# Strided attention: one store for two groups instead of one for each

## The chip, the cores and the metric

The kernel runs on one core of a Trainium2 chip. The metric is the device time of one execution in microseconds (us). The kernel before took 128.28 us, the median of three runs from 128.15 to 128.48.

## The reference

Every one of the 1024 queries of a head attends to the same 16 keys: positions 0, 64, 128, ... There are 8 x 12 = 96 heads with 64 elements per row, all in float32.

```python
attend_positions = np.arange(0, seq, stride)          # stride = 64, so 16 keys
q = Q[:, :, i:i + 1, :]
k = K[:, :, attend_positions, :]
v = V[:, :, attend_positions, :]
scores = np.einsum('bhqd,bhkd->bhqk', q, k) * scale   # scale = 1 / 8
weights = np.exp(scores - np.max(scores, axis=-1, keepdims=True))
weights = weights / (np.sum(weights, axis=-1, keepdims=True) + 1e-10)
result[:, :, i, :] = np.einsum('bhqk,bhkd->bhqd', weights, v)[:, :, 0, :]
```

Little is computed for each byte: 25.2 MB of Q are read, 25.2 MB of results are written, and of K and V only 0.8 MB together.

## The kernel before

The 96 heads are worked on in 24 groups of four heads. One group is 1 MiB of Q and 1 MiB of output. The four heads of a group follow one another in HBM.

For a group g the steps are these. `load(g)` brings Q into one of ten buffers `qn`; groups 0 and 1 come as 128 rows of 8 KiB, the others as 32 rows of 32 KiB. `cast(g)` turns it to bf16, half on GpSimd (L196) and half on ScalarE (L197). `transpose(g)` (VectorE, L206) turns 32 x 32 blocks of pairs. `scores(g)` is four matmuls (L219) and two exponentials on ScalarE (L231). `values(g)` lays the group's values out for the matmul (GpSimd, L184). `outputs(g, c)` with c = 0, 1, 2 multiplies weights and values (L247), takes the reciprocal of the sums (VectorE, L255) and scales into the output buffer: VectorE for c = 0 and 1 (L257), ScalarE and then GpSimd for c = 2 (L259, L260). The GpSimd instruction at L260 is the last one of a group. `store(g)` writes the group out.

In an output buffer a partition holds 8 KiB in a row: 4 x 8 rows of 64 elements, in all 2048 of float32. In HBM these 8 KiB are two pieces of 4 KiB, 512 KiB apart (pattern `[2 * SD, 2], [1, 16 * D]`). There are eight output buffers, so group g writes where group g-8 stood.

The order is written out by hand; no scheduler moves anything. In the loop, step g first runs `ahead(g)`: the transpose of group g+2, the scores of g+1, the values of g+2 and the cast of g+3. Then come the outputs of g, then `store(g)`, then `load(g + 10)`. The transpose of group g waits for the store of group g-10, since VectorE soon writes into that buffer.

All transfers are issued by SyncE (SP), in program order, on one queue: K, Q of group 0, V, Q of groups 1 to 9, and then store 0, load 10, store 1, load 11 and so on to store 13 and load 23, then stores 14 to 23 alone. An issue of a store waits for the L260 of its group; what stands behind it on SyncE waits with it. Completion is told by eight semaphores used in turn, so each issue also waits until the transfer eight issues earlier has landed.

Of the kernel before, what the change touches and what calls it, by code (L numbers as in the profile page):

```python
# [10 lines left out]
FP32 = mybir.dt.float32  # L11
# [6 lines left out]
def _ap_with(ap: bass.AP, new_ap, extra_offset: int = 0) -> bass.AP:  # L18
    return dataclasses.replace(
        ap, ap=[list(p) for p in new_ap], offset=ap.offset + extra_offset  # L20
    )


def _copy(nc, out: bass.AP, in_: bass.AP):

    sides = [
        mybir.BassSymbolicTensorAccessPattern(
            ap=side.ap, dtype=side.dtype, bass_ap=side,
            is_dma=True, for_custom_bir_dma=True,
        )  # L30
        for side in (in_, out)
    ]
    return nc.sync.add_instruction(
        mybir.InstDMACopy(
            name=nc.get_next_instruction_name(), engine=mybir.EngineType.SP,
            ins=sides[:1], outs=sides[1:], queue="qSPDynamicHW",
            mode="Copy",
        )
    )
# [9 lines left out]
def kernel(  # L49
# [10 lines left out]
    B, H, S, D = Q.shape  # L60
# [3 lines left out]
    P = 128  # L64
    HG = 4
    NG = B * H // HG
    NC = NG // 2
    SD = S * D
    KW = P + NK
    assert B * H == NG * HG and S == 1024 and D == 64 and NK == 16  # L70
    QBUFS = 10
    OBUFS = 8

    const = ctx.enter_context(tc.tile_pool(name="const", bufs=1))
# [12 lines left out]
    identity = const.tile([P, P], BF16, name="identity")  # L87
    qn_bufs = [const.tile([P, 32 * D], FP32, name=f"qn{i}") for i in range(QBUFS)]
    qb_bufs = [const.tile([P, 32 * D], BF16, name=f"qb{i}") for i in range(2)]
    out_bufs = [const.tile([P, 4, 8, D], FP32, name=f"out_sb{i}") for i in range(OBUFS)]  # L90
    kv_src = [[stride * D, P], [2 * HG * SD, NC], [1, D]]
    qn, stored, cast_by, scaled = {}, {}, {}, {}
    loaded, raised, masked = {}, {}, {}

    def implied(ins, earlier, why):
        tc.declare_no_dep(ins.ins, earlier.ins, reason=why)

    def load(g):
        qn[g] = qn_bufs[g % QBUFS]
        n = P if g < 2 else 32  # L100
        loaded[g] = _copy(nc, qn[g], _ap_with(Q, [[HG * SD // n, n], [1, HG * SD // n]], g * HG * SD))
        if g >= QBUFS:
            for earlier in (loaded[g - QBUFS], *cast_by[g - QBUFS]):
                implied(loaded[g], earlier, "the store before it has waited for both casts")
# [4 lines left out]
    for g in range(1, QBUFS):  # L109
# [13 lines left out]
        out=identity, in_=identity, compare_op=ALU.not_equal, fill=1.0, base=0,  # L123
# [3 lines left out]
    for c in range(2):  # L127
        for a in range(2):
            nc.gpsimd.tensor_copy(
                out=perm_v[:, c, a],  # L130
# [6 lines left out]
        out=s_sel, in_=identity.rearrange("p (h s k) -> p s h k", h=2, s=4),  # L137
# [10 lines left out]
    def key_rows(part):  # L148
        nc.scalar.copy(k_bf[:, part], k_raw[:, part])  # L149
        nc.vector.transpose(  # L150
            k_r[:, part].rearrange("p n d -> p (n d)").bitcast(I32),
            k_bf[:, part].rearrange("p n d -> p (n d)").bitcast(I32),
        )


    def keys(part, c, s):
        src, dst, col = 32 * (2 * c + s % 2), 32 * (2 * (s % 2) + s // 2), NK + 32 * s
        op = nc.gpsimd.tensor_copy if part is first and s >= 2 else nc.scalar.copy
        op(  # L159
            k_t[dst : dst + 32, 2 * part.start + c : 2 * part.stop : 2, :, col : col + NK],  # L160
            k_r[src : src + 32, part].rearrange(
                "p n (a k f) -> p a n f k", a=2, f=2
            )[:, s // 2],
        )


    def value_rows(n):
        vp = psum_o.tile([P, 3, 512], FP32, name="o_ps", tag="o")
        rows = vp[:, 0:2, 0 : NC // 2 * D].rearrange("p c (n d) -> p c n d", d=D)
        for c in range(2):  # L170
            nc.tensor.matmul(  # L171
                rows[:, c], lhsT=perm_v[:, c].rearrange("p a b e k -> p (a b e k)"),
                rhs=v_bf[:, 6 * n : 6 * n + 6], start=True, stop=True,
            )
        nc.vector.tensor_copy(  # L175
            out=v_rep[:, 6 * n : 6 * n + 6].rearrange("p n c d -> p c n d"), in_=rows
        )

    qb, qt, wt, vb, rec, out_sb = {}, {}, {}, {}, {}, {}
# [59 lines left out]

    def outputs(g, c):  # L240
        if c == 0:
            out_sb[g] = out_bufs[g % OBUFS]
            rec[g] = rec_pool.tile([P, 8, 4], FP32, name="rec", tag="rec")
        i0, n = ((0, 3), (3, 2), (5, 3))[c]
        ps = psum_o.tile([P, 3, 512], FP32, name="o_ps", tag="o")
        for i in range(n):
            nc.tensor.matmul(  # L247
                ps[:, i, 0 : 4 * D + 4], lhsT=wt[g][:, i0 + i], rhs=vb[g],
                start=True, stop=True,
            )  # L250
        r = rec[g][:, i0 : i0 + n]
        o = ps[:, 0:n, 0 : 4 * D].rearrange("p i (s d) -> p i s d", s=4)
        to = out_sb[g][:, :, i0 : i0 + n].rearrange("p s i d -> p i s d")
        by = r.unsqueeze(3).to_broadcast([P, n, 4, D])
        nc.vector.reciprocal(r, ps[:, 0:n, 4 * D : 4 * D + 4])  # L255
        if c < 2:
            nc.vector.tensor_tensor(out=to, in0=o, in1=by, op=ALU.mult)  # L257
        else:
            copied = nc.scalar.copy(to, o)  # L259
            scaled[g] = nc.gpsimd.tensor_tensor(out=to, in0=to, in1=by, op=ALU.mult)  # L260
            for past in range(g - OBUFS, -1, -OBUFS):
                for earlier in (stored[past], scaled[past]):
                    implied(copied, earlier, "VectorE has waited for the store")
                implied(scaled[g], stored[past], "VectorE has waited for the store")

    def store(g):
        o = out_sb[g]
        stored[g] = _copy(
            nc,
            _ap_with(out, [[16 * D, P], [2 * SD, 2], [1, 16 * D]], g * HG * SD),  # L270
            _ap_with(o, [o.ap[0], [1, 1], [1, 32 * D]]),
        )

    first, rest = slice(0, 4), slice(4, NC)
    key_rows(first)
# [15 lines left out]
    def ahead(g):  # L291
        if g + 2 < NG:
            transpose(g + 2)
        if g + 1 < NG:
            scores(g + 1)
        if g + 2 < NG:
            values(g + 2)
        if g + 3 < NG:
            cast(g + 3)

    for g in range(NG):
        if g > 0:
            ahead(g)
        for c in range(3):
            outputs(g, c)
        if g == 0:
            ahead(g)
        if g == 1:
            key_rows(rest)
        if 2 <= g < 6:  # L310
            for i in range(2 * g - 4, 2 * g - 2):
                keys(rest, i // 4, i % 4)
        if g == 4:
            value_rows(1)
        store(g)
        if g + QBUFS < NG:
            load(g + QBUFS)
# [1 line left out]
_INS = ['Q', 'K', 'V', 'stride']  # L319
_OUTS = [((8, 12, 1024, 64), 'float32')]  # L320
# [30 lines left out]
```

## Time and profile before

| | before |
|---|---|
| median of three runs | 128.28 us (128.15 to 128.48) |
| the profiled execution | 128.42 us |
| its span | 126.3 us |
| bytes moved | 51.19 MB, mean 405 GB/s over the span |
| busy: PE, DVE, ACT, POOL | 51%, 68%, 67%, 62% of the span |
| a Q load, issue to landing (median) | 14.8 us |
| a store, issue to landing (median) | 15.3 us |
| SyncE waiting before L33 | 37.7 + 24.9 + 12.6 + 12.1 us for GpSimd and transfers |

The profile is one execution. PE is TensorE, DVE is VectorE, ACT is ScalarE, POOL is GpSimd, SP is SyncE, and SPq is SyncE issuing. The span runs from the first to the last instruction; the 2.1 us that the execution takes beyond it lie around the program. A digit in the slices is the busy share of 3.2 us in tenths. A line of a window gives its bounds, its length, the busy time and count of each engine, the granted clock, the share of the 16 DMA engines' time that packets took (packets count in the window where they start, so it can pass 1), and the rate. A line of issues gives start, duration, engine, line, output and input. The number at the end of a line of DMA issues is the time from issue to landing.

Beside these views the trace keeps a record of every packet, with start, duration and size, and of every time that an engine's share of a transfer landed. Of the 7904 packets on the queue 3072 are K's and V's rows of 256 bytes, 800 are the 4-byte writes that tell of completion (16 for each of 50 transfers), 3328 have 8 KiB and 704 have 32 KiB.

### The profile page before, as it was taken

The numbers are of one execution on the slowest core, as the hardware profiler recorded it, in microseconds if no ns is written. First come the engines' busy times: TensorE is split into PE (matmuls) and PEld (weight loads), VectorE is DVE, ScalarE is ACT, GpSimd is POOL, SyncE is SP. The second block draws the span as 40 slices with busy tenths as digits, with TensorE's granted clock in tenths as the row PEclk, the third lists the DMA queues.
The fourth block names the chain that finished last, engine by engine and source line by source line (L and its number), as shares of the span: only waits on it lengthen the run. The fifth ranks groups of instructions, "written<-read, shape, count | busy, mean of one in ns | idle before, by whom it ended". The sixth has DMA issues, their size and how long they took to land.

```text
span 126.3 us, 1113 instructions
## 1 busy us (share of the span) xinstructions
PE 64.3 (51%) x292; PEld 29.8 (24%) x292; DVE 85.8 (68%) x151; ACT 84.5 (67%) x111; POOL 78.1 (62%) x89
## 2 busy tenths in 40 slices
PE   0005279294638776666464977636665459530000
PEld 0001033141313323333231433313333214210000
DVE  5931573659968879797997897979797973660000
ACT  4172807976999999979799768997979493530000
POOL 4084346736766876979979778796968775144000
PEclk9999999968997569999999657999999955965555
DMA  2999989999998998979999989989989899999991
GB/s 63 371 345 467 498 374 457 436 394 384 449 496 340 490 426 363 511 327 441 454 392 433 470 376 462 465 361 490 423 369 501 353 423 418 428 433 420 420 423 67
DMA packets 7910, 51.19 MB, mean 405 GB/s; under 512 B 3872, under 2 KB 3872, under 8 KB 3872
## 3 DMA queue, kind: packets, MB, share of 16 engines
q1 hardware_dynamic: 7904, 51.12, 97.0%
q8 instruction: 2, 0.03, 0.1%
q14 instruction: 4, 0.03, 0.1%
HBM read 25.95 MB, written 25.17 MB: 405 GB/s over the span
## 4 chain that ended last, share of the span: by engine, by line
DMA 37%; DVE 20%; ACT 11%; PE 9%; POOL 8%; issue 3%; SPq 1%; POOLq 1%; DVEq 0%
DMA qn<-in_Q_dram 37%; DVE out_sb L257 10%; DVE qt L206 6%; PE sc L219 4%; ACT out_sb L259 4%; PE o_ps L247 4%; POOL out_sb L260 3%; ACT w_all L231 3%; DVE rec L255 3%; ACT qb L197 3%; POOL qb L196 2%; POOL v_all L184 2%; POOLq L346 1%; DVE v_rep L175 1%; PE o_ps L171 1%
## 5 line engine op out<-in xcount | busy, mean ns | idle before, releaser
L247 PE MATMUL o_ps<-v_all,w_all 128*128 128x260 bf16 x192 | 38.3, 318 | 36.6 <-DVE out_sb L257 31.3
L260 POOL TENSOR_TENSOR out_sb<-out_sb,rec 128x768 f32<-128x768 f32 x24 | 35.3, 1472 | 27.2 <-ACT out_sb L259 27.2
L257 DVE TENSOR_TENSOR out_sb<-o_ps,rec 128x768 f32<-128x768 f32 (+1 forms) x48 | 39.6, 824 | 1.6
L231 ACT ACTIVATE w_all<-sc 64x512 bf16<-64x512 f32 x48 | 35.2, 734 | 5.2 <-PE sc L219 4.7
L206 DVE STREAM_TRANSPOSE qt<-qb 128x1024 int32<-128x1024 int32 x24 | 29.6, 1235 | 11.9 <-POOL qb L196 7.6
L219 PE MATMUL sc<-qt,k_t 128*128 128x512 bf16 x96 | 32.3, 470 | 9.9 <-DVE qt L206 9.9
L247 PEld LDWEIGHTS <-w_all 128*128 128x128 bf16 x192 | 18.8, 109 | 59.5 <-DVE out_sb L257 39.7
L259 ACT COPY out_sb<-o_ps 128x768 f32<-128x768 f32 x24 | 19.2, 799 | 16.3 <-DVE rec L255 15.7
L197 ACT CAST qb<-qn 128x1024 bf16<-128x1024 f32 x24 | 25.0, 1045 | 2.7 <-DMA qn<-in_Q_dram 2.2
L196 POOL CAST qb<-qn 128x1024 bf16<-128x1024 f32 x24 | 24.9, 1038 | 3.0 <-DMA qn<-in_Q_dram 2.9
L255 DVE RECIPROCAL rec<-o_ps 128x12 f32<-128x12 f32 (+1 forms) x72 | 15.0, 209 | 5.7 <-PE o_ps L247 5.2
L184 POOL TENSOR_TENSOR v_all<-mask,v_rep 128x256 bf16<-128x256 bf16 x24 | 16.0, 670 | 1.9 <-DVE v_rep L175 1.9
L219 PEld LDWEIGHTS <-k_t 128*128 128x128 bf16 x96 | 10.6, 111 | 19.9 <-POOL k_t L159 7.5
L159 ACT COPY k_t<-k_r 32x256 bf16<-32x256 bf16 (+1 forms) x12 | 4.4, 366 | 1.3 <-DVE k_r L150 1.1
L175 DVE CAST v_rep<-o_ps 128x768 bf16<-128x768 f32 x2 | 1.9, 958 | 4.6 <-PE o_ps L171 4.6
L133 DVE MEMSET k_t<- 128x3456 uint32 x1 | 2.9, 2938 | 1.5 <-PEq L332 1.5
L149 ACT CAST k_bf<-k_raw 128x256 bf16<-128x256 f32 (+1 forms) x2 | 1.0, 513 | 2.9 <-DMA k_raw<-in_K_dram 2.9
L140 POOL COPY v_all<-s_sel 128x12 bf16<-128x12 bf16 x1 | 0.2, 194 | 4.1 <-DVE s_sel L136 4.1
L171 PE MATMUL o_ps<-v_bf,perm_v 128*128 128x384 bf16 x4 | 1.3, 416 | 1.7 <-POOL v_bf L284 1.4
L149 ACT ACT_TABLE_LOAD x1 | 1.3, 1283 | 0.7 <-PEq L332 0.7
L150 DVE STREAM_TRANSPOSE k_r<-k_bf 128x128 int32<-128x128 int32 (+1 forms) x2 | 0.7, 370 | 1.4 <-ACT k_bf L149 1.4
L134 DVE MEMSET w_all<- 128x1536 uint32 x1 | 1.3, 1338 | 0.3 <-issue 0.3
(12 smaller groups left out, 4.6 us busy)
## 6 DMA issues: line engine op xcount, KB each, us to landing
qn<-in_Q_dram SPq DMA_DIRECT2D x24, 1024.0 KB, 14.8
out_dram<-out_sb SPq DMA_DIRECT2D x24, 1024.0 KB, 15.3
k_raw<-in_K_dram SPq DMA_DIRECT2D x1, 384.0 KB, 4.2
v_raw<-in_V_dram SPq DMA_DIRECT2D x1, 384.0 KB, 6.8
```

What stands on the lines that cost most here:

```text
L159: op(k_t[dst : dst + 32, 2 * part.start + c : 2 * part.stop : 2, :, col : col + NK], k_r[src : src + 32, part].rearrange("p n (a k f) -> p ...
L184: masked[g] = nc.gpsimd.tensor_tensor(out=vb[g][:, 0 : 4 * D].rearrange("p (s d) -> p s d", s=4), in0=mask, in1=v_rep[:, g // 2, g % 2].un ...
L196: nc.gpsimd.tensor_copy(out=qb[g][:, 0:half], in_=qn[g][:, 0:half]),
L197: nc.scalar.copy(qb[g][:, half:], qn[g][:, half:]),
L206: turned = nc.vector.transpose(qt[g].bitcast(I32), qb[g].bitcast(I32))
L219: nc.tensor.matmul(sc, lhsT=k_t[:, g, f, NK * (1 - e) : NK * (1 - e) + P], rhs=_ap_with(q, [q.ap[0], [D, 8], [16 * D, 2], [2, 32]], extra_ ...
L231: raised[g].append(nc.scalar.activation(out=_ap_with(wa, [wa.ap[0], [P, 8], [1, 2], [2, 32]], extra_offset=64 * a), in_=sc[64 * a : 64 * a ...
L247: nc.tensor.matmul(ps[:, i, 0 : 4 * D + 4], lhsT=wt[g][:, i0 + i], rhs=vb[g], start=True, stop=True,)
L255: nc.vector.reciprocal(r, ps[:, 0:n, 4 * D : 4 * D + 4])
L257: nc.vector.tensor_tensor(out=to, in0=o, in1=by, op=ALU.mult)
L259: copied = nc.scalar.copy(to, o)
L260: scaled[g] = nc.gpsimd.tensor_tensor(out=to, in0=to, in1=by, op=ALU.mult)
```

## The change

The eight output buffers become four of two groups each: a partition holds 16 KiB in a row, the lower group first. Group 0 lies alone in the second half of the first buffer, then come the pairs (1,2), (3,4) to (21,22), and group 23 lies alone in a first half. Still a group writes where the group eight before it stood.

A pair is stored by one transfer of 2 MiB, after its second group is done: 128 rows of 16 KiB out of the buffer, in HBM four pieces of 4 KiB each, 512 KiB apart. The two loads of the pair follow it. So the queue is now store 0, load 10, store (1,2), loads 11 and 12, and so on to store (11,12), loads 21 and 22, store (13,14), load 23, four more pairs and store 23. There are 39 transfers in place of 50. The eight semaphores still limit how many are under way.

```diff
-    out_bufs = [const.tile([P, 4, 8, D], FP32, name=f"out_sb{i}") for i in range(OBUFS)]
+    out_bufs = [const.tile([P, 2, 4, 8, D], FP32, name=f"out_sb{i}") for i in range(OBUFS // 2)]
...
-            out_sb[g] = out_bufs[g % OBUFS]
+            out_sb[g] = out_bufs[(g + 1) // 2 % (OBUFS // 2)][:, (g + 1) % 2]
...
-    def store(g):
-        o = out_sb[g]
-        stored[g] = _copy(
+    def store(lo, hi):
+        n, pair = hi + 1 - lo, out_bufs[(hi + 1) // 2 % (OBUFS // 2)]
+        o = pair[:, (lo + 1) % 2]
+        done = _copy(
             nc,
-            _ap_with(out, [[16 * D, P], [2 * SD, 2], [1, 16 * D]], g * HG * SD),
-            _ap_with(o, [o.ap[0], [1, 1], [1, 32 * D]]),
-        )
+            _ap_with(out, [[16 * D, P], [2 * SD, 2 * n], [1, 16 * D]], lo * HG * SD),
+            _ap_with(o, [o.ap[0], [1, 1], [1, n * 32 * D]]),
+        )
+        for g in range(lo, hi + 1):
+            stored[g] = done
...
-        store(g)
-        if g + QBUFS < NG:
-            load(g + QBUFS)
+        if g % 2 == 0 or g == NG - 1:
+            lo = max(g - 1, 0) if g % 2 == 0 else g
+            store(lo, g)
+            for past in range(lo, g + 1):
+                if past + QBUFS < NG:
+                    load(past + QBUFS)
```

Nothing is changed in the instructions of the other engines, other than the place in memory that the outputs are written to and the stores that the transposes wait for.

## The prediction

> **What bounds the kernel now.** I read the page's slices and queue table first, then transfer rates in windows, then SyncE's issues and the end of the chain of waits.
>
> ```profile
> span 126.3 us, 1113 instructions
> ...
> DMA  2999989999998998979999989989989899999991
> ```
> ```profile
> q1 hardware_dynamic: 7904, 51.12, 97.0%
> ...
> qn<-in_Q_dram SPq DMA_DIRECT2D x24, 1024.0 KB, 14.8
> out_dram<-out_sb SPq DMA_DIRECT2D x24, 1024.0 KB, 15.3
> ```
>
> The reader is to see that the 16 DMA engines hold packets of this one queue for 97.0% of the span (122.5 us), while no compute engine passes 68%. Taking the trace's packet records one by one, all 16 engines hold a packet from 2 to 123 us; the first starts at 1.84, the last ends at 124.98. So the time is the packets' sum. A change helps if it shortens that sum and hurts if it lets the queue run dry; work on the compute engines counts only through when it releases transfers.
>
> ```profile
> core 0: us, PE busy (x) PEld busy (x) DVE busy (x) ACT busy (x) POOL busy (x), PEclk, DMA share, GB/s
> 13.00:27.00 14.00, 8.56 (x29) 3.51 (x29) 8.70 (x14) 8.63 (x11) 7.10 (x9) 0.96 1.01 433
> 103.00:115.00 12.00, 6.12 (x25) 2.51 (x23) 6.62 (x16) 4.87 (x7) 6.05 (x5) 0.64 1.01 425
> ```
>
> The first window holds only loads of 32 rows of 32 KiB, the second only stores of 128 rows of 8 KiB. At the same share the short rows move 2% less.
>
> ```profile
> 21.42 0.63 SPq L33 DMA_DIRECT2D out_dram<-out_sb  x1
> 22.10 0.60 SPq L33 DMA_DIRECT2D qn<-in_Q_dram  x1
> 28.87 0.59 SPq L33 DMA_DIRECT2D out_dram<-out_sb  x1
> 29.51 0.69 SPq L33 DMA_DIRECT2D qn<-in_Q_dram  x1
> 33.91 0.59 SPq L33 DMA_DIRECT2D out_dram<-out_sb  x1
> ...
> 42.24 0.59 SPq L33 DMA_DIRECT2D out_dram<-out_sb  x1
> ```
> ```profile
> 81.22 19.52 DMA qn<-in_Q_dram
> ...
> 110.72 1.47 POOL out_sb L260
> 112.20 1.48 issue
> 113.68 1.51 POOLq L346
> ```
>
> The first list has stores 0, 1 and 2 and their loads: early on SyncE issues when a group is done. The second says that the last load lands at 100.74, that group 22 is done at 112.20 and group 23 at 115.2; store 23 is issued there and lands 10 us later, behind three others.
>
> **The change, part by part.** *Packets.* Eleven pairs are stored as rows of 16 KiB. In the packet records an 8 KiB store packet takes 311 ns (median) and a 32 KiB load packet 1219 ns from 55 us on: four starts against one cost 4 x 311 - 1219 = 25 ns, 8.3 ns a start. The windows agree: 425 and 433 GB/s over 16 engines at 1.01 are 311.5 and 305.7 ns per 8 KiB, and 5.8 ns is three quarters of a start of 7.7 ns. An engine has 8 of a store's 128 rows, so 88 starts fall away: 88 x 8.3 = 0.73 us. No row shows a 16 KiB packet. The upper end is the rate of the 32 KiB packets, 176 x 5.8 = 1.02 us. The lower end is below nothing: an HBM row of a store is 4 KiB, so a 16 KiB packet jumps three times where two of 8 KiB jump once each, and 8 KiB stores at 311 against the one-piece 8 KiB loads at 309 give 2 ns a jump: 88 x 2 = 0.18 us lost if nothing is merged. I take 0.73, because the 32 KiB load is also a packet of four pieces on its far side, the nearest form.
>
> A rule prices the same step lower. The Trainium skill (DMA: Bandwidth & Descriptors, Why small descriptors are slow) gives about three cycles of overhead per packet; at the 850 MHz of its section Where 436 GB/s comes from that is an estimated 3.5 ns, so 88 x 3.5 = 0.31 us, and the sum would be 0.4 us higher, about 128.1. The 8.3 ns of this trace disagree, so I keep those.
>
> *Completion writes.* Each transfer ends in one 4-byte packet per engine, 9 ns in the records. Eleven fewer: 0.10 us.
>
> *SyncE.* Eleven issues of 0.59 us go. SyncE spends 88 us of the span in waits before L33, so this is worth nothing on the path; the queue behind it is what covers it.
>
> *Store g waits for g+1 (g odd), and so do its load and everything behind it on SyncE.* The worst place is the first pair. Load 10, issued at 22.10, lands at 35.68 on its last engine and about 35.0 on its first; by the records the engines are free from 34.68 to 35.32. Before, store 1 and load 11 (29 us) were queued behind it. Now nothing is until store (1,2) at 33.91, when group 2 is done. How long from issue to first packet on an empty queue? One row: K is issued at 0.74 and its first packet starts at 1.84, 1.10 us. With SyncE's 0.59 for a store instead of K's 0.43 it is 1.26, so about 35.2. An engine idles 0 to 0.5 us; bound above by K's landing at 4.2 us less its 1.73 us of packets and 0.4 of landing, 2.1 us from issue, which is 36.0 and a gap of 0.7 to 1.3 us. Below, nothing. I take 0.2 us, the nearest row being K's start.
>
> The next pair: from 35.2, a pair (16 x 0.307 = 4.9 us) and loads 11 and 12 (2.44 each) run to 45.0. Group 4 is done at 42.24 and its store starts by 43.5. Ahead by 1.5 us, then 2.6 at group 6, and more after, since groups finish every 3.3 to 4.3 us and transfers need 4.9 a group. So this happens once.
>
> *Loads.* Load 10+g of an odd g now stands behind store g+1: 2.46 us later in the queue; even ones keep their place. Casts come long after their loads until about load 20, so those delays are covered. The last, load 23, is odd: it lands 2.46 later less 0.5 us saved on seven pairs by then, near 102.7. The chain after it is rigid (11.5 us to group 22, 14.4 to group 23): 114.2 and 117.1.
>
> *The end.* Store (21,22) is issued at 114.2 and starts by 115.5. The store ahead of it, (19,20), ends where store 20 did less about 0.7: 115.0 on the first engine and 116.9 on the last (records: 115.70 and 117.59). The early engines may idle 0.5 us, but they had 1.5 us to spare on the late one that sets the end. Store 23 comes at 117.1, before (21,22) ends at 119.9 or later. Cost nothing; that cover goes if the first packet needs 2.7 us.
>
> *Buffers.* Still eight groups deep. The transpose of group g waits for the store of g-10, which for odd g now lands with its partner; but in the queue that store still stands ahead of load g, which the same transpose needs. Nothing.
>
> *Sum.* 128.42 (the profiled execution, span 126.3 and 2.1 around it) - 0.73 - 0.10 + 0.20 = 127.8. That execution was 0.14 above the median of 128.28, so against the median 127.65 us.
>
> **Rivals.** *No merging.* If the packets stay at 8 KiB, or the far side's 4 KiB pieces are what costs, 0.10 is gained, up to 0.18 lost, 0.2 lost to the gap: 128.2 to 128.6. For it: the store's HBM rows are 4 KiB. Against: today's packets are 8 KiB, the buffer's row and not the 4 KiB one.
>
> *The queue runs dry* at (1,2), the one that ends slower. Each us that the first packet comes after 35.3 is paid by all engines. The gain of 0.83 is used up when it comes near 36.1, 2.2 us after issue; beyond 36.5 the kernel is slower by over 0.3%. At the 36.0 bound it gives 128.28 - 0.83 + 0.7 to 1.3 = 128.2 to 128.8. Against: K started in 1.10 us. For: that was a load with nothing in flight, and no store has been seen on an empty queue.
>
> *Four pieces half a MiB apart per packet* go slower than two of two. If each of two added jumps cost as much as a packet's start, a packet takes 622 + 17 ns and 88 x 17 = 1.5 us are lost: 128.28 + 1.5 - 0.1 + 0.2 = 129.9. Against: 311 and 309 ns for two pieces and one. The Trainium skill (DMA: Bandwidth & Descriptors, Latency and other measured facts) has copies at a row pitch of 512 KiB at 207 GB/s against 214 with a padded pitch; the stores of this trace already step by 512 KiB and keep 425.
>
> **How the numbers follow.** Merging with a small gap 0.64 (with both unknown costs 128.28 - 1.12 = 127.16 to 128.28 - 0.83 + 0.5 = 127.95), no merging 0.13, dry queue 0.15, slow pieces 0.08. The runs before spread 128.15 to 128.48, so 0.3%, 0.38 us, is what can be told: the first case is faster but for 0.05; no merging is the same, with 0.02 slower; dry splits into 0.08 same and 0.07 slower; slow pieces are slower but for 0.02. Faster 0.59, same 0.26, slower 0.15. The range goes from the low end of the first case, with the runs' scatter 127.1, to 128.7, which takes in no merging and most of the dry case.
>
> **What would show it.** Right: packets of the queue fall from 7904 to 7904 - 1408 - 176 = 6320, the window of pure stores moves 427 to 430 GB/s, the queue's time falls by 0.8 us, the slices near 35 us stay at 9, load 23 lands near 102.7. Wrong: 7728 packets (no merging), a slice under 8 near 35 us (dry), or under 425 GB/s in the last stores (slow pieces).

## The result and the profile after

The changed kernel takes 131.57 us, the median of four runs from 130.73 to 131.84, beside 128.33 us for four runs of the kernel before. The ratio is 1.0236, with a 95% interval from 1.0205 to 1.0267: slower by 2.4%. The forecast was 127.65 us, and 131.57 lies above its range.

The page after, in the lines that answer to those shown of before:

```profile
span 129.7 us, 1090 instructions
...
DMA  2999999999799979999999989989989999998990
```
```profile
q1 hardware_dynamic: 6320, 51.12, 95.3%
...
qn<-in_Q_dram SPq DMA_DIRECT2D x24, 1024.0 KB, 15.2
out_dram<-out_sb SPq DMA_DIRECT2D x11, 2048.0 KB, 14.9
out_dram<-out_sb SPq DMA_DIRECT2D x2, 1024.0 KB, 9.8
```

The packets fell to 6320, just as forecast, so the rows did become 16 KiB. But 95.3% of 129.7 us are 123.6 us of packets an engine, against 122.5 before: 1584 packets fewer (1408 rows and 176 completion writes), and over 1 us more. The profiled execution took 131.84 us, 3.42 more than that of before; its last packet ends at 128.38 in the packet records, 3.40 later than before, so all of the loss lies in the transfers.

The rates in three stretches say where. The columns are as in the windows shown before: the last two are the DMA share and GB/s. First the kernel before, then the changed one.

```profile
34.00:46.00 12.00, 8.55 (x37) 3.85 (x35) 9.54 (x16) 11.69 (x18) 8.70 (x9) 0.73 0.95 403
46.00:70.00 24.00, 13.75 (x79) 6.93 (x78) 21.29 (x40) 21.52 (x27) 20.10 (x21) 0.99 1.01 425
70.00:100.00 30.00, 18.88 (x95) 9.20 (x93) 25.78 (x49) 24.83 (x31) 24.09 (x24) 0.89 1.01 426
```
```profile
34.00:46.00 12.00, 7.21 (x40) 3.27 (x38) 10.63 (x20) 11.45 (x18) 8.45 (x10) 0.98 0.93 350
46.00:70.00 24.00, 14.94 (x72) 7.18 (x72) 20.12 (x38) 21.45 (x28) 19.66 (x20) 0.86 0.99 413
70.00:100.00 30.00, 16.97 (x84) 8.37 (x84) 23.39 (x43) 22.30 (x29) 21.33 (x21) 0.88 1.01 423
```

Between 34 and 46 us the changed kernel moves 53 GB/s less, 0.64 MB or 1.5 us of work at 425 GB/s. Between 46 and 70 it is 12 GB/s, 0.7 us. The DMA share falls by only 0.02 in both, so most of this is not an idle queue: packets take longer. (The share counts a packet that is held up as busy.)

SyncE's issues of the changed kernel (start, duration, engine, line, output and input):

```profile
22.04 0.60 SPq L33 DMA_DIRECT2D qn<-in_Q_dram  x1
34.23 0.59 SPq L33 DMA_DIRECT2D out_dram<-out_sb  x1
34.86 1.96 SPq L33 DMA_DIRECT2D qn<-in_Q_dram  x2
42.78 0.59 SPq L33 DMA_DIRECT2D out_dram<-out_sb  x1
```

Store (1,2) is issued at 34.23, and by the packet records its first packet starts at 35.48; the engines had been free since 34.56 to 35.16, so the mean engine idles 0.67 us. (The records name no engine. Figures for one engine come from putting packets in chains, each starting where another has just ended.) Then comes what was not forecast. The first six packets of the store on each engine take 608 to 648 ns (616 is the median of 16 KiB packets), the last two up to 1199, and then load packets of 32 KiB, usually 1213 to 1219 ns, take up to 1765. Over the whole kernel, 73 of 704 load packets pass 1260 ns (18 before), in sum 23 us beyond 1218 ns each; long 16 KiB packets add 14 us. Summed over 16 engines that is 2.3 us for each, and some engines carry more than others.

The end of the chain of waits:

```profile
81.95 24.74 DMA qn<-in_Q_dram
...
116.54 1.47 POOL out_sb L260
118.01 1.49 issue
119.50 1.50 POOLq L352
```

Load 23 lands at 106.70, where 102.7 was forecast, and groups 22 and 23 end 11.3 and 14.3 us behind it, at 118.0 and 121.0. Store (21,22) is issued at 118.04, when the first engine has been through with (19,20) since 117.65, so the early engines idle a second time, some 0.7 us on the mean. The latest engine, which sets the end, is never idle there: it leaves (19,20) at 121.01, 3.4 us behind the first (1.9 before).

### The profile page after: what moved, and what is told of

It reads as the page before. It is cut to its first block, busy times and chain, and to the rows that moved or that the text cites. A ratio compares the mean times of both kernels' runs of the same rounds, so it can differ in the third digit from the quotient of the medians.

```text
span 129.7 us, 1090 instructions
## 1 busy us (share of the span) xinstructions
PE 67.5 (52%) x292; PEld 31.1 (24%) x292; DVE 86.1 (66%) x151; ACT 84.7 (65%) x111; POOL 78.1 (60%) x89
## 3 DMA queue, kind: packets, MB, share of 16 engines
q1 hardware_dynamic: 6320, 51.12, 95.3%
## 4 chain that ended last, share of the span: by engine, by line
DMA 26%; DVE 22%; ACT 18%; PE 11%; POOL 10%; issue 3%; SPq 1%; POOLq 1%; DVEq 0%
DMA qn<-in_Q_dram 26%; DVE out_sb L257 11%; DVE qt L206 7%; ACT out_sb L259 6%; ACT w_all L231 5%; PE o_ps L247 5%; PE sc L219 5%; ACT qb L197 5%; POOL out_sb L260 5%; DVE rec L255 3%; POOL qb L196 3%; POOL v_all L184 2%; ACT k_t L159 2%; POOLq L352 1%; DVE v_rep L175 1%
## 5 line engine op out<-in xcount | busy, mean ns | idle before, releaser
L247 PE MATMUL o_ps<-v_all,w_all 128*128 128x260 bf16 x192 | 40.0, 331 | 39.3 <-DVE out_sb L257 29.9
L219 PE MATMUL sc<-qt,k_t 128*128 128x512 bf16 x96 | 33.7, 487 | 9.9 <-DVE qt L206 9.9
L247 PEld LDWEIGHTS <-w_all 128*128 128x128 bf16 x192 | 19.4, 113 | 63.1 <-DVE out_sb L257 38.6
L259 ACT COPY out_sb<-o_ps 128x768 f32<-128x768 f32 x24 | 19.2, 798 | 15.8 <-DVE rec L255 15.6
L219 PEld LDWEIGHTS <-k_t 128*128 128x128 bf16 x96 | 11.3, 117 | 21.0 <-issue 8.3
```

Of the source, the lines that this page charges most:

```text
L219: nc.tensor.matmul(sc, lhsT=k_t[:, g, f, NK * (1 - e) : NK * (1 - e) + P], rhs=_ap_with(q, [q.ap[0], [D, 8], [16 * D, 2], [2, 32]], extra_ ...
L247: nc.tensor.matmul(ps[:, i, 0 : 4 * D + 4], lhsT=wt[g][:, i0 + i], rhs=vb[g], start=True, stop=True,)
```

## The experiments

Three theories were put to test. A: the queue runs empty near 35 and 118 us, and the restart brings the long packets. B: packets of 16 KiB in four pieces hold up the loads beside them. C: two loads back to back bring the long packets; the kernel before alternates one store and one load. In all of them the ratio is to the kernel before on the same chip (128.4 to 128.5 us).

**Order without delay.** Each group is stored alone again; only the order of the changed kernel stays, two stores and then two loads. SyncE issues store 1 when group 1 is done (29.10 us), so nothing is delayed but the first load of a pair.

```diff
-            store(lo, g)
+            for one in range(lo, g + 1):
+                store(one, one)
```

> The order and the delay of the changed kernel, but each group stored by its own transfer of 8 KiB rows: both stores of a pair when its second group is done, then both loads. Theory A (the queue runs empty near 35 us and near 118 us, and the long packets follow from all engines restarting together): as slow as the changed kernel, 131 to 132 us, with an empty stretch of 0.5 us or more near 35 us and single load packets of over 1.4 us after it. Theory B (packets of 16 KiB in four pieces hold up the loads beside them): only the empty stretches stay, 0.7 us each on the mean engine, so 129.0 to 129.7 us, and no more long load packets than before (18).

Measured: 130.15 us, ratio 1.0132 (1.0098 to 1.0166). The expected stop was not there, since store 1 is not held: the engines are not idle between 4 and 124 us. Still 56 load packets are long, with 15.8 us of excess. They fall on both loads of a pair, with three quarters of the excess (11.9 us) on the second. So theory A is not all of it, and B cannot be, since no packet has 16 KiB. That gave theory C.

The excess is 1.0 us an engine, and by the records of completion the mean engine's last share lands 0.8 us later than in the kernel before. The last engine's lands 1.9 us later, and that one sets the time. Why it is so far behind is seen in the page's queue table, in a row that is the same for both kernels:

```profile
q8 instruction: 2, 0.03, 0.1%
```

These are two packets of 16 KiB of instructions. In both kernels the first, near 48 us, takes its place between two packets of the queue on one engine, for 1.18 us before and 1.03 here, and that engine is the last from then on to the end. Here it also has 2.9 us of long packets, the most of all engines, against 0.8 before: together 2.0 us more, where the end came 1.9 us later.

**The rows in 8 KiB, all else as changed.** 256 bytes between the two groups keep the rows apart.

```diff
-    out_bufs = [const.tile([P, 2, 4, 8, D], FP32, name=f"out_sb{i}") for i in range(OBUFS // 2)]
+    out_bufs = [const.tile([P, 2, 33, D], FP32, name=f"out_sb{i}") for i in range(OBUFS // 2)]
...
-            _ap_with(o, [o.ap[0], [1, 1], [1, n * 32 * D]]),
+            _ap_with(o, [o.ap[0], [33 * D, n], [1, 32 * D]]),
```

> As the changed kernel, one transfer for two groups issued at the same place, but the two groups lie 256 bytes apart in the buffer, so that the rows are 8 KiB again. Theory A: 131 to 132.5 us, the empty stretches are the same and the 0.7 us of packet starts are not saved. Theory B: 129 to 130 us, because the packets are those of the kernel before.

Measured: 131.56 us, ratio 1.0244 (1.021 to 1.0277), as expected by theory A, with 75 long load packets and again 350 GB/s from 34 to 46 us. The changed kernel's median is 131.57, but its runs spread over 1.1 us, so that the two agree to 0.01 us is chance. No gain or harm of the rows' length is seen: theory B falls. For the 0.73 us that were to be gained the pace of packets, further down, is the sharper test.

**No stop, merged pairs.** The loads are issued two groups earlier.

```diff
-            for past in range(lo, g + 1):
+            for past in range(lo + 2 if g else 0, g + 3):
```

> Merged pairs of 16 KiB rows as in the changed kernel, but every load after the first ten is issued two groups earlier: loads 10, 11, 12 after store 0, loads 13, 14 after store (1,2) and so on; the queue then holds 4.9 us more work at 35 us and load 23 comes before store (13,14). Theory A: no empty stretch, load 23 near 96 us, and the 0.8 us of the prediction are gained: 127.3 to 127.9 us. Theory B: the 16 KiB packets are all there, so the long load packets stay and only 0.7 to 1.4 us come back: 130 to 131 us.

Measured: 129.55 us, ratio 1.0066 (1.0032 to 1.0099). The queue is not empty near 35 us. 2.0 us come back, more than the 0.7 to 1.4 of theory B, but not all that theory A expected. Loads still come in twos (and three after store 0), and 41 load packets are long with 12.3 us of excess.

**Single groups up to 6**, then pairs:

```diff
-        if g % 2 == 0 or g == NG - 1:
-            lo = max(g - 1, 0) if g % 2 == 0 else g
+        if g % 2 == 0 or g == NG - 1 or g < 7:
+            lo = g - 1 if g % 2 == 0 and g > 6 else g
```

> Groups 0 to 6 stored alone, each followed by its load, as before; pairs of 16 KiB rows from (7,8) to (21,22), group 23 alone. Theory A: the queue is not empty near 35 us, no restart, few long packets; the end has load 23 2.5 us late as predicted: 127.5 to 128.3 us. Theory B: eight of eleven pairs still hold up loads, the pairs beside loads being (7,8) to (13,14), so about 130 us, with long load packets between 60 and 100 us.

Measured: 128.94 us, ratio 1.0037 (1.0018 to 1.0056). No stop near 35 us, and before 70 us only four long load packets. Those that come, 29 with 9.5 us of excess, lie at 70 us and later, where loads come in twos; near 116 us the mean engine idles 0.2 us. It costs half a us still, against the gain that theory A expected, and 1 us less than theory B did.

**Delay without the order.** The pair goes out in rows of 16 KiB after its second group, as even and odd partitions, each half followed by one load. The transposes wait for both halves.

```diff
...
-            store(lo, g)
-            for past in range(lo, g + 1):
+            parts = [slice(0, P, 1)] if lo == g else [slice(0, P, 2), slice(1, P, 2)]
+            for past, part in zip(range(lo, g + 1), parts):
+                store(lo, g, part)
```

> As the changed kernel, still only after the second group of a pair and in rows of 16 KiB, but a pair goes out as two transfers of 1 MiB, one of the even and one of the odd partitions, and each is followed by one of the two loads: store half, load, store half, load, as the kernel before alternates. Theory C (two loads back to back, with all engines reading for 5 us, bring the long load packets): the long packets fall to about the 18 of before, the empty stretch near 35 us stays, and the time is 128.4 to 129.2 us. Theory A (the empty stretch and the restart after it bring them): they stay near 73 and the time is 131 to 132 us.

Measured: 130.2 us, ratio 1.0137 (1.012 to 1.0155), between the two expectations. The stop is there (0.51 us on the mean engine) and so is a burst of long packets right behind it: 13.8 us of excess in the first stores and 16.0 us in load 11. After that, with one store and one load in turn, loads 12 to 23 have 2 us of excess, no more than the kernel before. So there are two causes: a burst after the stop, and long loads where two of them stand in a row.

**Delay alone, in 8 KiB rows** shows the same without halves. The first store of a pair is held until the second group is done; one store and one load in turn.

```diff
-            lo = max(g - 1, 0) if g % 2 == 0 else g
-            store(lo, g)
-            for past in range(lo, g + 1):
+            for past in range(max(g - 1, 0) if g % 2 == 0 else g, g + 1):
+                store(past, past)
+                if past < g:
+                    tc.add_manual_dep(
+                        stored[past].ins, scaled[g].ins.name,
+                        mybir.DependencyInfo(mybir.DependencyClass.Sync, mybir.DependencyReason.ANTI),
+                        reason="held until the second group of the pair is done",
+                    )
                 if past + QBUFS < NG:
                     load(past + QBUFS)
```

> Delay alone: groups stored one by one in rows of 8 KiB, store and load in turn as in the kernel before, but the first store of each pair is held until the second group of the pair is done. If the stop of the queue near 35 us and its restart are what the delay costs: 129.8 to 130.4 us, as with the halves, with 20 us or more of excess in packets between 35 and 46 us. If the halves or their 16 KiB rows had a part in those 1.8 us: under 129.5 us.

Measured: 130.89 us, ratio 1.0182 (1.0164 to 1.02), half a us above the expected range, so the halves and their rows had no part in the loss. Its three stretches:

```profile
34.00:46.00 12.00, 6.87 (x38) 3.28 (x38) 10.76 (x20) 11.62 (x18) 8.63 (x10) 1.00 0.98 355
46.00:70.00 24.00, 14.38 (x75) 7.19 (x76) 20.89 (x39) 21.65 (x28) 19.91 (x21) 0.93 0.98 413
70.00:100.00 30.00, 16.77 (x94) 8.45 (x92) 23.95 (x45) 23.19 (x30) 22.67 (x22) 0.97 1.02 434
```

The packets are those of the kernel before, in its order; only their time differs, and the stretch from 34 to 46 us falls from 403 to 355 GB/s. By the packet records store 1 starts at full pace after the stop; then, on all 16 engines, its last two packets take some 300 ns more than 311 and the one before them 97 to 261 more, and 14 of the 16 second packets of load 11 take 1936 to 2211 ns in place of 1218. From 35 to 45 us that is 13.2 us of excess in stores and 14.1 in loads, 1.7 us an engine; with 0.40 us of idle time 2.1 of the 2.4 us that were lost.

**The transfers alone.** Is it the engines at work beside the transfers? Four kernels leave all computation out: the output buffers are zeroed once, and the zeros are stored. Each ran once, so their times stand for one execution. First the changed kernel's order and rows. Of its loop this is left:

```diff
+    for buf in out_bufs:
+        nc.vector.memset(buf, 0.0)
...
     for g in range(NG):
-        if g > 0:
-            ahead(g)
-        for c in range(3):
-            outputs(g, c)
...
         if g % 2 == 0 or g == NG - 1:
```

> All transfers of the changed kernel in its order (pairs in rows of 16 KiB, then two loads), and no computation: the output buffers are zeroed once and stored, the result is not attention. The queue is never empty. If two loads in a row or the 16 KiB rows alone make packets long, some 40 to 75 load packets over 1260 ns and 125 to 126 us of span are seen here too. If they need the compute engines at work beside them: fewer than 15 long load packets and a span near 123.5 us (1.8 before the first packet, 121.6 of packets).

Measured: 128.36 us, span 126.6 us (125 to 126 was expected), 71 long load packets with 25.6 us of excess. From 18 us on, when the zeros are written, no engine but SyncE works. The long packets need no computation.

Alone again, in the order of the kernel before and in 8 KiB rows:

```diff
-        if g % 2 == 0 or g == NG - 1:
...
+        store(g, g)
+        if g + QBUFS < NG:
+            load(g + QBUFS)
```

> All transfers and no computation again (zeroed buffers are stored), but each group stored alone in rows of 8 KiB and followed by its load, the order of the kernel before. If two loads in a row are what makes load packets long: at most 25 load packets over 1260 ns (71 in the pairs' order) and a mean load packet near 1222 ns (1253). If the transfers alone run like that in any order: 50 to 75 long ones again.

Measured: 7 long load packets, 1.8 us of excess, a mean load packet of 1219 ns against 1253: theory C holds for the packets. (Rows and order change together here; that the rows are not the cause is seen above, where two stores of 8 KiB rows and two loads had 56.) But the time is 128.37 us, the same as in pairs. Alone, the longer packets of the pairs' order did not reach the end: the mean engine's last share lands 0.9 us later, as with computation, but the last engine's at the same time, since the engines then leave their last store within 1.5 us of one another instead of 2.1. These kernels fetch no instructions meanwhile. The span of 126.6 us without any computation also says that the kernel before, with 126.3, takes no longer than its transfers alone.

Then with one stop, store 1 held by four more fills of its buffer:

```diff
+    for _ in range(4):
+        nc.vector.memset(out_bufs[1], 0.0)
```

> As the run before it, alternating and without computation, but store 1 is held by the vector engine until about 35 us, so that the queue runs empty once, near 35 to 36 us, as in the changed kernel. If a stop costs only its empty time: 0.3 to 1.0 us on the mean engine and no more long packets than without the stop. If the restart itself makes packets long (in the kernels with computation 25 to 37 us summed over the 16 engines): 15 us or more in excess, that is 1 us or more a mean engine, within the 10 us after the restart.

The two runs from 34 to 46 us (columns: bounds, length, DVE and POOL busy, clock, DMA share, GB/s), without and with the stop:

```profile
34.00:46.00 12.00, 0.00 (x0) 0.00 (x0) 1.00 0.97 410
```
```profile
34.00:46.00 12.00, 1.39 (x1) 0.00 (x0) 1.00 0.84 295
```

Measured: 130.13 us, 1.76 more. The engines idle 1.8 us on the mean (from about 34.9 to 36.7 us), and the restart adds 13.4 us of excess in store packets and 14.1 in load 11, the same amount as with computation, 1.7 us an engine: 115 GB/s over 12 us, 3.2 us of work in all. Not all of it reaches the end, because the engines then end in step, where without the stop the last is 2.1 us behind the first.

Alone, in the pairs' order, with loads 10 to 23 in rows of 8 KiB:

```diff
-        n = P if g < 2 else 32
+        n = P if g < 2 or g >= QBUFS else 32
```

> The transfers of the changed kernel alone, in the pairs' order, but loads 10 to 23 go in 128 rows of 8 KiB instead of 32 of 32 KiB. If the long rows of the loads are what suffers: few load packets over 331 ns and an excess under 5 us over all engines (25.6 us with long rows). If any two loads in a row suffer: 15 us or more in excess, spread over shorter packets.

Measured: 128.03 us, 13.0 us of excess in 8 KiB packets of which 2.0 lie in the first ten us: half of what the long rows had, between the two expectations. The same with computation, and its control, the kernel before with such loads (the same edit):

> Order alone, with other load rows: two stores of 8 KiB rows, then two loads, as in the run that cost 1.75 us, but loads 10 to 23 in 128 rows of 8 KiB. If long rows of the loads are what two loads in a row hold up: 128.3 to 129.2 us. If any two loads in a row cost it: 129.8 to 130.4 us.

> Control for the run before it, and a candidate: the kernel before with loads 10 to 23 in rows of 8 KiB. If the form of the load rows is neutral in this order: 128.3 to 128.6 us. If a packet start costs the 8 ns that the prediction took from loads against stores: 14 loads x 6 more packets an engine x 8 ns = 0.7 us slower, 129.1 us. If rows alike in length on both sides run better together: under 128.2 us.

Measured: 129.67 us, ratio 1.0101 (1.0042 to 1.0159), for the order, and 128.47 us, ratio 1.0004 (0.9988 to 1.002), for the control. The order costs in both forms of the loads; whether it costs less with short rows the intervals do not tell. The control tells more: 14 loads with 6 packets more on each engine, 84 starts, cost nothing that can be seen. At 8.3 ns each they would have cost 0.7 us. The control's expectation of 129.1 us for such a price failed; that of a neutral form held.

**Versions meant to win.** Halves alternating with loads, the loads two groups earlier:

```diff
-                if past + QBUFS < NG:
-                    load(past + QBUFS)
+                for more in range(QBUFS if g == 0 else past + QBUFS + 2, past + QBUFS + 3):
+                    if more < NG:
+                        load(more)
```

> The same halves of 16 KiB rows alternating with loads, and the loads two groups earlier, so that the queue does not run empty near 35 us and load 23 comes sooner. Theory C: nothing of the loss is left and the shorter packet sum shows, 127.4 to 127.9 us. Theory A: also without a loss, 127.4 to 128.0 us; with the run before the two together tell whether either cause is missing. If neither holds (the delay of the stores itself costs): 129 us or more.

Measured: 128.37 us, ratio 0.9999 (0.9971 to 1.0027). With stop and double loads both gone (but for loads 10 to 12) the loss of time is gone, and the gain that both theories expected does not come: the mean engine has 0.3 us less of recorded packet time than in the kernel before, and idles 0.7 us near 116 us. Part of the evenness is luck. The span is 126.6 us (median), 0.3 longer than before, and the time outside the span is 1.8 us in place of 2.1, in all runs of this kernel, for a reason not found. With the loads only one group earlier and whole pairs after the last load:

> Meant to beat both: rows of 16 KiB as even and odd halves alternating with loads, the loads one group earlier (loads 10 and 11 after store 0), and whole pairs only once the loads are out. No empty stretch near 35 us, no two loads in a row after load 11, and load 23 before store (13,14). Order and stop as causes: 127.5 to 128.1 us, from 88 packet starts fewer at 6 to 8 ns each. If shorter packet sums do not reach the end of the span: 128.2 to 128.7 us.

Measured: 129.13 us, ratio 1.0064 (1.0037 to 1.009), above both expectations. It has no stop and few long loads (22, 7.0 us), and its last packet ends at 125.23 us, 0.25 later than in the kernel before. Of the rest of its 0.65 us 0.3 lie outside the span, where its ten runs have 2.4 to 2.5 us and those of the kernel before 2.1 to 2.2, and some 0.15 between the last packet and the end of the span; what takes them is open. Last, pairs only where no load is left:

```diff
-        if g % 2 == 0 or g == NG - 1:
-            lo = max(g - 1, 0) if g % 2 == 0 else g
+        if g < 15 or g % 2 == 0 or g == NG - 1:
+            lo = g - 1 if g > 14 and g % 2 == 0 else g
             store(lo, g)
-            for past in range(lo, g + 1):
-                if past + QBUFS < NG:
-                    load(past + QBUFS)
+            if g + QBUFS < NG:
+                load(g + QBUFS)
```

> The kernel before up to store 14 and load 23, one store and one load in turn; only groups 15 to 22, stored when no load is left, go as four pairs of 16 KiB rows. Neither a stop of the queue nor two loads in a row, nor a load that comes later. If the two are the whole loss and the shorter packet sum is real: 4 pairs x 8 packet starts x 6 to 8 ns and 4 completion writes, 0.2 to 0.3 us faster, 128.0 to 128.3 beside 128.4 to 128.5. If the saved starts never reach the end: 128.3 to 128.6 us.

Measured: 128.77 us, ratio 1.0023 (1.0006 to 1.004), above both expectations. No stop, no double loads, no late load, and no gain. In the profiled execution the last packet ends 0.18 us later than before and the span 0.37 us later still behind it; why stays open. It also gives the price of a packet start without anything else. By the records of completion, an engine needs 19.63 us for its four pairs, from the end of store 14 to that of (21,22). The kernel before needs 19.69 for the same eight groups. That is 15 ns a pair, 9 of which are the completion write, and about 1 ns for each of eight packet starts. No version beat the kernel before.

## Why the prediction was wrong, point by point

*What bounds the kernel.* That the 16 engines' packets are the time was right. "So the time is the packets' sum" was then used with fixed durations for each size, and this is the step that failed: the same packets take longer after a stop (1.7 us an engine, beyond the gap) and in another order (1.0 us an engine, and by itself 1.75 us of time). That a stop also costs what comes after it, and that two loads in a row cost anything, was in no term. The late engine that sets the end, which the prediction saw, also falls further behind.

*Packets, 0.73 us.* The count came out as forecast, the gain did not: 15 ns a pair, 0.17 us with the completion writes, and none that a time shows (131.57 against 131.56 us). The 8.3 ns came from comparing stores of short rows with loads of long ones, as if the row were all that differs. It is the direction that differs: with the transfers alone, undisturbed loads come every 2.43 us in rows of 32 KiB (loads 2 to 8) and in rows of 8 KiB (load 18 behind load 17, the median engine), and stores of 8 KiB rows every 2.46. Durations were also the wrong measure. An 8 KiB store packet lasts 311 ns, but eight stores took 19.69 us, 2.461 each, so a packet begins every 307 ns: neighbours overlap. The changed kernel's pairs (15,16) to (19,20) come at 4.91 us each, 2 x 2.46. So its last stores are not slow pieces either, though the window from 108 to 117 us shows 422 GB/s, under the 425 named as the sign of that rival: 2 MiB in 4.91 us are 427. The Trainium skill's rule of about three cycles a packet (DMA: Bandwidth & Descriptors, Why small descriptors are slow), set aside in the prediction for the 8.3 ns, gave an estimated 3.5 ns: nearer than the row that was preferred, and by these runs still too much for packets of 8 KiB.

*The first stop.* Its place was right, and so was the first packet, 1.25 us after the issue (1.26 forecast). The gap was 0.67 us, where 0.2 were taken and 0.7 to 1.3 given as the bound above; store (1,2) was itself issued 0.3 us later than the 33.91 assumed. The slice of 7 near 35 us is the sign that was named for a dry queue. No second stop came in the first half. The term was short of the restart, 1.7 us an engine where the delay was tested alone. It was listed as the rival that ends slower, with 0.15 and at most 128.8 us, and that price held only the wait for the first packet.

*Loads.* Load 23 was to be 2.46 us later in the queue, less what was saved. It came 6.0 us later, at 106.70, since the packets ahead of it had become longer and the engines had stood idle once. The chain behind it was rigid, as said (11.3 and 14.3 us).

*The end.* With load 23 late, store (21,22) was issued at 118.04 instead of 114.2, and the cover of the early engines was used up. The end itself is set by the latest engine, as the prediction has it.

*Buffers and SyncE* cost nothing, as said: in the whole trace no compute engine waits for a store, and SyncE only waits.

*The sum of causes.* Order alone costs 1.32%, delay alone 1.82%, both together, as changed, 2.36%, and with neither (halves, loads two earlier) no time, though 0.3 us of span. The parts overlap, and each was shown by itself. What was not settled is the mechanism below: why the packets behind a restart, and second loads, take longer. Computation is excluded for both, the length of the stores' rows too; the addresses, the order in which transfers are made ready for the engines, and the step in which the engines run were not told apart.

## What to carry to other kernels

Where a queue of transfers is the bound, look for the first place where the queue holds less than a merged transfer waits for its second half. Here the price at that place was not the gap alone but the restart. Keep loads and stores alternating as they were when timing a change of transfer sizes, or the order is measured along with it. Price a packet by how far apart completions lie, not by the recorded duration, and compare like with like: stores with stores. Look at the last engine as well as at the mean one, and at the span as well as at the time.

## What the runs showed that was not expected

- A stop of the queue of 0.4 to 1.8 us made the packets behind it longer by 1.7 to 1.9 us an engine, with and without computation; the burst ends within 10 us.
- Two stores and then two loads made 56 to 75 load packets of 704 longer than 1260 ns, against 7 to 18 with one of each in turn and no stop, and this alone cost 1.3% in the kernel with computation; with the transfers alone the longer packets did not move the end (128.36 against 128.37 us).
- One fetch of 16 KiB of instructions, 1.0 to 1.2 us on one engine near 48 us, made that engine the last one up to the end, in the kernel before and in the one with the order alone.
- The length of a row, from 8 KiB up, hardly changed the pace of this queue: a MiB of stores took 2.46 us in rows of 8 and of 16 KiB, and 84 more packet starts an engine in the loads gave a ratio of 1.0004 (0.9988 to 1.002).
